# A split activation tile, two more load buffers, a new order of K pairs and exchanged bank kinds in the down projection of a decoder layer

## The chip, the core and the metric

One core of one Trainium2 chip computes one layer of a hybrid decoder for 256 tokens. The metric is the device time of one execution in microseconds, as the median of several. TensorE (PE in the profile) multiplies, VectorE (DVE) and ScalarE (ACT) prepare operands and drain results, GpSimd (POOL) moves small pieces by DMA, and SyncE (SP) issues the weight loads.

## The reference

All arrays are float32. Sizes: 256 tokens, width 2048, feed-forward width 5632. The layer has four parts:

```python
z = rms_norm(x, mix_norm_g) @ w_in                 # 2048 -> 8208, feeds mLSTM heads and forgetting attention
x = x + concat([A, B]) @ w_out                     # 2048 -> 2048
u = rms_norm(x, ffn_norm_g) @ w_up                 # 2048 -> 2 * 5632
a, g = split(u, 2)
a = causal_dwconv(a, conv_w, conv_b)               # width 3
x = x + (gelu(a) * g) @ w_down                     # 5632 -> 2048
gate = sigmoid(rms_norm(x, ple_norm_g) @ w_ple_gate)
x = x + gate * (p @ w_ple_proj)
```

The change touches the last three products: up, down, and gate with proj.

## The kernel before

**Products in three matmuls.** Each float32 operand is kept as a rounded part (hi) and the rest (lo), both in the type fp32r. A product is hi x hi, hi x lo and lo x hi, three matmuls into one PSUM bank (lines 996 to 998 for down, 1235 to 1237 for up, 311 to 313 for the gate). Weights arrive as raw float32 tiles of 128 x 1024; ACT casts hi (line 947), DVE subtracts it for lo (line 948). This pair of steps is a *split* (`part`, line 946).

**Activations.** The transposed, split activations are tiles `aT` of 16 K tiles x 512 columns (hi 256, lo 256). `new_aT` (line 357) gives them out from one pool with two slots: `hT`, `catT`, `x2T`, `uA`, then `w2`, then `x3T`, so `w2` takes the slot of `x2T`, the input of up, and `x3T` that of `uA`.

**Units.** From the up stage on everything runs as a list of units (`Unit`, line 922; `run_units`, line 953). A unit has loads (SP), a split, and matmuls. Loads are issued as long as raw buffers are free (`free_raws`, `new_raw`), splits as long as pairs of hi and lo buffers are. Up has 11 groups of 16 units (`up_group`), one unit per K tile, 12 matmuls each. Its result is drained to `EZ` by ACT (line 853), transposed by DVE into `Y` (line 191), moved back to `EZ` by 16 POOL DMAs (line 197), and goes through the convolution, GELU and gate product in pieces hung behind later units (`up_act`, lines 865 to 880); the last group's pieces run behind units 5 to 9 of down.

**Down.** Each half of 1024 output columns goes through 44 K tiles in 22 pairs (`down`, line 977). A *plain* pair is two units (`eight`) of one load and 12 matmuls. A *seven-product* pair (`seven`, for the nine pairs of `SEVEN`) does a 2 x 2 block product with seven products instead of eight: two loads, four units of 3, 6, 6 and 6 matmuls, four 512-wide subtractions in place on the raw tiles (lines 1044, 1045, 1054, 1055), and sums of the left blocks, S, that were written to DRAM in the up stage and are loaded again (line 1027). Its two raw tiles are free only after its fourth split. The plain products of a half are gathered in four banks (`X_tag`), P1, P5, P6 and P7 in four others (`P_tag`); `sums_done` adds the latter to the residual behind the last seven-product pair, `add_rest` the former at the end.

**Buffers.** In the up stage there are 3 raw tiles and 4 pairs of hi and lo. From the first unit of down on there are also: raw `pT` (one, from the pool of the left sums), and, once the last convolution has left them, `EZ` (two) and a part of `Y` (`ring`, one); and in `w2` three more pairs of hi and lo and two places for S. PSUM has 8 banks, 4 of the kind "mm" and 4 of "aux". Up groups alternate between the kinds, down exchanges them between its halves, and the gate and proj products and the transposes of `x3T` use one kind each.

**Order.** The program order is not the final one on an engine: a scheduler reorders instructions within the dependencies when the program is built. Each engine then works its list in order, and so does SP's queue.

Of the kernel before, what the change touches and what calls it, by code (L numbers as in the profile page):

```python
# [9 lines left out]
F32 = mybir.dt.float32  # L10
F32R = mybir.dt.float32r
# [4 lines left out]
P = 128  # L16
S = 256
NT = S // P
D = 2048
KD = D // P  # L20
# [4 lines left out]
KF = FF // P  # L25
# [6 lines left out]

BLK = 1024
RAW, PARTS = 3, 4
PARTS2 = 3

SEVEN = (2, 4, 6, 8, 10, 12, 14, 16, 18)
AHEAD_DMA, AHEAD_SPLIT = 3, 3
PAD = 16


LO_SHIFT = 16
LAST_UP = 9


@with_exitstack
def layer_kernel(
# [19 lines left out]
    def bank(tag, name):  # L67
        return ps.tile([P, 512], F32, tag=tag, name=name)
# [283 lines left out]
        act.copy(dst, b[:, 256:512])  # L352
        dve.tensor_add(dst, b[:, 0:256], dst)

    aT = {}

    def new_aT(name):
        aT["cur"] = apool.tile([P, KD, 512], F32R, tag="aT", name=name, bufs=2)
        return aT["cur"]

    all_k = list(range(0, KD, 2))

# [438 lines left out]
    with tc.tile_pool(name="ffn", bufs=1) as fp:  # L801
# [98 lines left out]
        def new_raw(j, name):  # L900
            tag = free_raws(j)[0]
            taken.append(tag)
            used[tag] = len(used) and max(used.values()) + 1
            if tag == "ring":
                return ring[:, 0:2].rearrange("p a b -> p (a b)")
            if tag in ("e0", "e1"):
                return EZ[:, int(tag[1])]
            if tag == "raw":
                return wp.tile([P, BLK], F32, tag="raw", name=name, bufs=RAW)
            return fp.tile([P, BLK], F32, tag=tag, name=name, bufs=room[tag])  # L910

        def new_parts(j, shift):
# [40 lines left out]
        def run_units(us, first_late, gate):  # L953
            loaded = split = 0
            for i, u in enumerate(us):
                if i == first_late:
                    w2 = new_aT("w2").rearrange("p k n -> p (k n)")
                    v = w2[:, 0 : 6 * BLK].rearrange("p (u n) -> p u n", n=BLK)
                    room.update(pT=1, e0=1, e1=1, ring=1)
                    late.update(gate=gate, free=i + LAST_UP, hi=v[:, 0:3], lo=v[:, 3:6],  # L960
                                S=w2[:, 6 * BLK :].rearrange("p (b i c) -> p b i c", b=2, c=256))
                more = i >= first_late
                now[0] = i
                while True:
# [12 lines left out]
        def down(c0, X_tag, P_tag, sums_done, done, at):  # L977

            banks, seen, us = {}, {}, []
            pairs = range(KF // 2)
            plain = [p_ for p_ in pairs if p_ not in SEVEN]
            total = {"P1": len(SEVEN), "P5": len(SEVEN), "P6": len(SEVEN), "P7": len(SEVEN)}
            for t in range(NT):
                for n in range(2):
# [80 lines left out]

            for p_ in pairs:
                if p_ in SEVEN:
                    us.extend(seven(p_, sums_done if p_ == SEVEN[-1] else None))  # L1070
# [57 lines left out]
        def x3_columns(*ks):  # L1128
            return lambda *_: [column(x3s[k // 4], k % 4, get_x3T()[:, k], g_ple[:, k : k + 1]) for k in ks]

        def transposes(*ks, tag="aux"):
            return lambda *_: [transpose_x(get_x3T(), k0, g_ple, tag) for k0 in ks]

        pT = {}
# [41 lines left out]
        def last_group(c0, n):  # L1176
# [44 lines left out]
        def up_group(q):  # L1221
# [29 lines left out]
        us += down(1024, "aux", "mm", sums_done(1024), add_rest(1024),  # L1251
                   {23: x3_squares(0), 27: x3_squares(1),
                    31: x3_columns(0, 1, 2, 3), 35: x3_columns(4, 5, 6, 7)})
# [48 lines left out]
```

## Time and profile before

| | |
|---|---|
| median of three runs | 1263.54 us (1263.43 to 1263.77) |
| profiled execution | 1263.79 us, span 1262.1 us |
| mean granted TensorE clock | 0.997 |
| DMA | 271.27 MB, 215 GB/s on average |
| matmuls of up, by line 1235 | 704, 389 ns each as listed (they overlap) |

Rows of a time line give start, duration, engine, line, operation and out<-in; in brackets the idle time before the instruction and what ended it. "x4" merges four neighbours. Rows by stretch give, after the stretch, its length, then busy us (and instructions) of PE, PEld (weight load), DVE, ACT and POOL, the granted clock, the busy share of the 16 DMA engines and GB/s. SPq rows are issues of DMAs. Since matmuls overlap, the distance between starts says more than the duration.

### The profile page before, as it was taken

The page shows a single profiled execution, that of the slowest core. Times are in us where ns is not written, and L with a number is a line of the kernel's source. Part 1 is how long each engine was busy: PE and PEld are TensorE (multiplying, and loading weights), DVE is VectorE, ACT ScalarE, POOL GpSimd, SP SyncE. Part 2 cuts the span into 40 slices and gives each one's busy share as a digit, 9 for nine tenths or more (in the row PEclk, how much of TensorE's full clock was granted, in tenths as well). Part 3 has the DMA queues.
Part 4 walks back from the last instruction along what each step waited for, and adds up shares of the span by engine and source line. Part 5 has one row for each costly group of instructions (what it writes and reads, how often), then busy time and mean ns, then how long its engine had stood idle before and what let it go on. Part 6 is the DMA issues. An engine that isn't in the chain of part 4 may idle for free.

```text
span 1262.1 us, 16487 instructions
## 1 busy us (share of the span) xinstructions
PE 1247.4 (99%) x5887; PEld 1051.9 (83%) x5887; DVE 831.6 (66%) x1055; ACT 684.1 (54%) x964; POOL 210.4 (17%) x395
## 2 busy tenths in 40 slices
PE   9999999999999999999999999999998999999998
PEld 7899988888888788888888888888876888888887
DVE  6455668744565645665676567657668998899653
ACT  7655555545454544665565556546545555556542
POOL 2003035100213202202211220222020000050000
PEclk9999999999999999999999999999998999999999
DMA  8667767656666757777877887787786785877670
GB/s 257 183 181 207 222 189 203 198 157 171 200 194 214 210 182 218 210 231 211 253 219 219 244 233 225 226 235 232 228 238 234 256 325 190 263 249 232 190 237 35
DMA packets 133476, 271.27 MB, mean 215 GB/s; under 512 B 14007, under 2 KB 28977, under 8 KB 133393
## 3 DMA queue, kind: packets, MB, share of 16 engines
q1 hardware_dynamic: 119936, 246.51, 64.8%
q0 software_dynamic: 13072, 23.53, 6.4%
q8 instruction: 46, 0.75, 0.3%
q14 instruction: 37, 0.30, 0.1%
q10 hardware_dynamic: 385, 0.16, 0.0%
HBM read 246.54 MB, written 6.83 MB: 201 GB/s over the span
## 4 chain that ended last, share of the span: by engine, by line
PE 94%; DMA 2%; DVE 2%; ACT 1%; issue 0%; SPq 0%; ACTq 0%; DVEq 0%
PE up L1235 13%; PE up L1237 13%; PE up L1236 13%; PE tg L312 10%; PE tg L311 10%; PE tg L313 10%; PE wg L343 5%; PE wg L344 2%; DMA raw<-in_w_down_dram 1%; PE dnP L997 1%; PE dnP L998 1%; PE dnP L996 1%; PE dn(0, 1)_8857 L996 1%; PE dn(0, 0)_8853 L996 1%; PE dn(1, 0)_8861 L996 1%; PE dn(1, 0)_8861 L998 1%
## 5 line engine op out<-in xcount | busy, mean ns | idle before, releaser
L948 DVE TENSOR_TENSOR lo<-raw,hi 128x1024 fp32r<-128x1024 f32 x235 | 284.4, 1214 | 185.7 <-ACT hi L947 185.0
L947 ACT CAST hi<-raw 128x1024 fp32r<-128x1024 f32 x235 | 244.3, 1045 | 247.5 <-DMA raw<-in_w_up_dram 118.5
L282 DVE TENSOR_TENSOR lo<-raw,hi 128x1024 fp32r<-128x1024 f32 (+2 forms) x161 | 178.2, 1112 | 149.1 <-ACT hi L280 148.8
L1237 PE MATMUL up<-hi,x2T 128*128 128x512 f32 x704 | 273.9, 389 | 0.0
L1236 PE MATMUL up<-lo,x2T 128*128 128x512 f32 x704 | 273.9, 389 | 0.0
L1235 PE MATMUL up<-hi,x2T 128*128 128x512 f32 x704 | 269.6, 389 | 1.3 <-DVE x2T L139 1.3
L280 ACT CAST hi<-raw 128x1024 fp32r<-128x1024 f32 (+2 forms) x161 | 153.7, 960 | 150.3 <-PE tg L313 77.5
L1235 PEld LDWEIGHTS up<-hi,x2T 128*128 128x128 f32 x704 | 132.2, 188 | 28.8 <-DVE x2T L139 1.5
L1237 PEld LDWEIGHTS up<-hi,x2T 128*128 128x128 f32 x704 | 132.1, 188 | 27.6
L1236 PEld LDWEIGHTS up<-lo,x2T 128*128 128x128 f32 x704 | 132.1, 188 | 27.4
L312 PE MATMUL tg<-lo,hT 128*128 128x512 f32 (+1 forms) x384 | 136.8, 357 | 0.0
L311 PE MATMUL tg<-hi,hT 128*128 128x512 f32 (+1 forms) x384 | 135.6, 358 | 0.0
L313 PE MATMUL tg<-hi,hT 128*128 128x512 f32 (+1 forms) x384 | 135.5, 354 | 0.0
L197 POOL DMA_DIRECT2D EZ<-Y x176 | 93.1, 536 | 171.1 <-DVE Y L191 140.0
L343 PE MATMUL wg<-hT,hi 128*128 128x512 f32 x256 | 90.2, 399 | 0.0
L312 PEld LDWEIGHTS tg<-lo,hT 128*128 128x128 f32 x384 | 72.2, 188 | 7.7 <-DVE lo L282 0.5
L313 PEld LDWEIGHTS tg<-hi,hT 128*128 128x128 f32 x384 | 72.1, 188 | 7.5
L311 PEld LDWEIGHTS tg<-hi,hT 128*128 128x128 f32 x384 | 71.7, 188 | 7.1
L344 PE MATMUL wg<-hT,lo 128*128 128x256 f32 x256 | 70.1, 283 | 0.0
L947 ACT CAST w<-raw 128x1024 fp32r<-128x1024 f32 (+1 forms) x41 | 40.5, 998 | 34.0 <-DMA raw<-in_w_down_dram 12.6
L948 DVE TENSOR_TENSOR w<-raw,w 128x1024 fp32r<-128x1024 f32 (+1 forms) x41 | 46.9, 1153 | 14.2 <-ACT w L947 14.0
L343 PEld LDWEIGHTS wg<-hT,hi 128*128 128x128 f32 x256 | 47.5, 188 | 9.1
(633 smaller groups left out, 1963.0 us busy)
## 6 DMA issues: line engine op xcount, KB each, us to landing
raw<-in_w_up_dram SPq DMA_DIRECT2D x176, 512.0 KB, 4.9
raw<-in_w_in_dram SPq DMA_DIRECT2D x79, 512.0 KB, 4.1
raw<-in_w_down_dram SPq DMA_DIRECT2D x55, 512.0 KB, 6.3
raw<-in_w_in_dram SPq DMA_DIRECT2D x48, 344.0 KB, 3.5
raw<-in_w_out_dram SPq DMA_DIRECT2D x32, 512.0 KB, 4.7
EZ<-Y POOLq DMA_DIRECT2D x176, 64.0 KB, 5.4
EZ<-in_w_down_dram SPq DMA_DIRECT2D x22, 512.0 KB, 5.9
raw<-in_w_ple_gate_dram SPq DMA_DIRECT2D x20, 512.0 KB, 5.3
```

The source lines that it names most:

```text
L280: act.copy(hi, raw[:, :w])
L282: dve.tensor_sub(lo, raw[:, :w], f32(hi))
L311: pe.matmul(o, ah, hi[:, i, :], start=first, stop=False)
L312: pe.matmul(o, ah, lo[:, i, :], start=False, stop=False)
L313: pe.matmul(o, al, hi[:, i, :], start=False, stop=last)
L343: pe.matmul(o, h[:, i, cols], a, start=first, stop=False)
L344: pe.matmul(o[:, 256:512], l[:, i, cols], a[:, 0:256], start=False, stop=last)
L947: act.copy(hi, raw)
L948: dve.tensor_sub(lo, raw, f32(hi))
L1235: pe.matmul(o, ah, hi[:, n], start=k == 0, stop=False)
L1236: pe.matmul(o, ah, lo[:, n], start=False, stop=False)
L1237: pe.matmul(o, al, hi[:, n], start=False, stop=k == KD - 1)
```

## The change

- `aT` tiles are made of two tiles, K tiles 0 to 11 (tag `aTa`) and 12 to 15 (`aTb`), each with two slots (class `Tiles`).
- `w2` takes a slot of `aTa` alone: two pairs of hi and lo (`PARTS2` 2 instead of 3) and two places for S.
- A slot of `aTb` becomes two raw buffers of the new tag `late`, from the first unit of down to the end.
- The first half of down goes through its pairs in the order `FIRST`, with the plain pairs 0, 1, 3, 5 ahead of the first seven-product pair; the second half keeps its order. `last7` names the pair behind which `sums_done` runs.
- The bank kinds "mm" and "aux" are exchanged from the first up group on, through down, the transposes of `x3T`, `pT`, gate and proj.
- `EZ` and `ring` may be used as raw buffers from one unit later.

```diff
-PARTS2 = 3
+PARTS2 = 2
+FIRST = (0, 1, 3, 5, 2, 7, 4, 6, 9, 8, 11, 10, 13, 12, 15, 14, 17, 16, 19, 18, 20, 21)
+FRONT = 12
...
-        aT["cur"] = apool.tile([P, KD, 512], F32R, tag="aT", name=name, bufs=2)
-        return aT["cur"]
+    class Tiles:
+        def __init__(self, name):
+            self.a = apool.tile([P, FRONT, 512], F32R, tag="aTa", name=name, bufs=2)
+            self.b = apool.tile([P, KD - FRONT, 512], F32R, tag="aTb", name=name + "b", bufs=2)
+        def __getitem__(self, idx):
+            k = idx[1]
+            if isinstance(k, slice):
+                v, o = (self.a, 0) if k.stop <= FRONT else (self.b, FRONT)
+                k = slice(k.start - o, k.stop - o)
+            else:
+                v, o = (self.a, 0) if k < FRONT else (self.b, FRONT)
+                k -= o
+            return v[(idx[0], k, *idx[2:])]
...
+            if tag == "late":
+                if tag not in late:
+                    late[tag] = apool.tile([P, 2, BLK], F32, tag="aTb", name="w2raw", bufs=2)
+                    late["n"] = 0
+                late["n"] += 1
+                return late[tag][:, late["n"] % 2]
...
-                    w2 = new_aT("w2").rearrange("p k n -> p (k n)")
-                    v = w2[:, 0 : 6 * BLK].rearrange("p (u n) -> p u n", n=BLK)
-                    room.update(pT=1, e0=1, e1=1, ring=1)
-                    late.update(gate=gate, free=i + LAST_UP, hi=v[:, 0:3], lo=v[:, 3:6],
-                                S=w2[:, 6 * BLK :].rearrange("p (b i c) -> p b i c", b=2, c=256))
+                    v = apool.tile([P, 6, BLK], F32R, tag="aTa", name="w2", bufs=2)
+                    room.update(late=2, pT=1, e0=1, e1=1, ring=1)
+                    late.update(gate=gate, free=i + LAST_UP + 1, hi=v[:, 0:2], lo=v[:, 2:4],
+                                S=v[:, 4:6].rearrange("p b (i c) -> p b i c", c=256))
...
-        def transposes(*ks, tag="aux"):
+        def transposes(*ks, tag="mm"):
...
-            bk = bank("aux", "pTp")
+            bk = bank("mm", "pTp")
...
-                    st[key] = bank("mm", f"tl{t}{c}")
+                    st[key] = bank("aux", f"tl{t}{c}")
...
-                        st["b"] = {(t, n): bank("mm" if q % 2 else "aux", f"up{t}{n}") for n in range(2) for t in range(NT)}
+                        st["b"] = {(t, n): bank("aux" if q % 2 else "mm", f"up{t}{n}") for n in range(2) for t in range(NT)}
...
-        us += down(0, "mm", "aux", sums_done(0), add_rest(0), {})
-        us += down(1024, "aux", "mm", sums_done(1024), add_rest(1024),
+        us += down(0, "aux", "mm", sums_done(0), add_rest(0), {}, FIRST)
+        us += down(1024, "mm", "aux", sums_done(1024), add_rest(1024),
...
-            g_ = (units(token_group(w_ple_gate, all_k, get_x3T, c0, n, gate_done(c0, n)))
+            g_ = (units(token_group(w_ple_gate, all_k, get_x3T, c0, n, gate_done(c0, n), tag="aux"))
...
-            p_ = units(token_group(w_ple_proj, [0], lambda: pT["t"], c0, n, proj_done, tag="aux"))
+            p_ = units(token_group(w_ple_proj, [0], lambda: pT["t"], c0, n, proj_done, tag="mm"))
```

More of the change, by code (lines that the diff above doesn't have):

```diff
@@ L353, in merge @@
         dve.tensor_add(dst, b[:, 0:256], dst)
-    aT = {}
+    class Tiles:
[11 more added lines that the diff above has]
+            return v[(idx[0], k, *idx[2:])]
     def new_aT(name):
-        aT["cur"] = apool.tile([P, KD, 512], F32R, tag="aT", name=name, bufs=2)
-        return aT["cur"]
+        return Tiles(name)
     all_k = list(range(0, KD, 2))
@@ L975, in run_units, with down @@
                 u.fn(*u.parts)
-        def down(c0, X_tag, P_tag, sums_done, done, at):
+        def down(c0, X_tag, P_tag, sums_done, done, at, pairs):
             banks, seen, us = {}, {}, []
-            pairs = range(KF // 2)
             plain = [p_ for p_ in pairs if p_ not in SEVEN]
+            last7 = [p_ for p_ in pairs if p_ in SEVEN][-1]
             total = {"P1": len(SEVEN), "P5": len(SEVEN), "P6": len(SEVEN), "P7": len(SEVEN)}
@@ L1069, in down @@
                 if p_ in SEVEN:
-                    us.extend(seven(p_, sums_done if p_ == SEVEN[-1] else None))
+                    us.extend(seven(p_, sums_done if p_ == last7 else None))
                 else:
@@ L1249, in layer_kernel @@
         first_late = len(us)
-        us += down(0, "mm", "aux", sums_done(0), add_rest(0), {})
-        us += down(1024, "aux", "mm", sums_done(1024), add_rest(1024),
+        us += down(0, "aux", "mm", sums_done(0), add_rest(0), {}, FIRST)
+        us += down(1024, "mm", "aux", sums_done(1024), add_rest(1024),
                    {23: x3_squares(0), 27: x3_squares(1),
-                    31: x3_columns(0, 1, 2, 3), 35: x3_columns(4, 5, 6, 7)})
+                    31: x3_columns(0, 1, 2, 3), 35: x3_columns(4, 5, 6, 7)}, range(KF // 2))
         for c0, n in ((0, 512), (512, 512), (1024, 512), (1536, 512)):
-            g_ = (units(token_group(w_ple_gate, all_k, get_x3T, c0, n, gate_done(c0, n)))
+            g_ = (units(token_group(w_ple_gate, all_k, get_x3T, c0, n, gate_done(c0, n), tag="aux"))
                   if c0 < D - n else last_group(c0, n))
-            p_ = units(token_group(w_ple_proj, [0], lambda: pT["t"], c0, n, proj_done, tag="aux"))
+            p_ = units(token_group(w_ple_proj, [0], lambda: pT["t"], c0, n, proj_done, tag="mm"))
             if c0 == 0:
```

## The prediction

> **What bounds the kernel now.** I read the page first, then busy time by stretches, then the instructions of each engine around the two stretches in which TensorE is not full.
>
> ```profile
> span 1262.1 us, 16487 instructions
> PE 1247.4 (99%) x5887; PEld 1051.9 (83%) x5887; DVE 831.6 (66%) x1055; ACT 684.1 (54%) x964; POOL 210.4 (17%) x395
> ...
> 400.00:500.00 100.00, 98.45 (x437) 80.98 (x437) 53.69 (x57) 47.09 (x60) 21.32 (x40) 1.00 0.70 207
> ...
> 900.00:950.00 50.00, 46.99 (x202) 37.40 (x201) 36.44 (x43) 26.81 (x32) 9.04 (x17) 1.00 0.77 233
> 950.00:1000.00 50.00, 45.56 (x184) 35.86 (x184) 43.71 (x53) 26.47 (x30) 0.00 (x0) 0.93 0.75 256
> 1000.00:1050.00 50.00, 50.00 (x222) 41.40 (x221) 45.16 (x51) 29.34 (x37) 0.00 (x0) 1.00 0.74 261
> ```
>
> PE is busy 1247.4 of 1262.1 us, so the change can only win what lies in gaps and at a slow clock. The rows by stretch place them: 1.55 us at the start of the up stage (400 to 500), and 3.01 + 4.44 us between 900 and 1000, where the granted clock (third figure from the end) also drops to 0.93. From 1000 on PE is full again. The instructions show the same in time:
>
> ```profile
> 434.26 0.39 PE L313 MATMUL tg<-hi,catT 128*128 128x512 f32 x1
> 434.94 1.25 PE L147 MATMUL xT<-ident,xs 128*128 128x128 f32 x8 [0.29 <-DVE xs L769]
> 437.45 0.50 PE L1235 MATMUL up<-hi,x2T 128*128 128x512 f32 x1 [1.26 <-DVE x2T L139]
> ...
> 916.30 0.39 PE L996 MATMUL dn(0, 0)_7993<-hi,uA 128*128 128x512 f32 x1
> 916.53 0.39 PE L997 MATMUL dn(0, 0)_7993<-lo,uA 128*128 128x512 f32 x1
> ...
> 939.76 0.50 PE L996 MATMUL dn(0, 0)_7993<-w,uA 128*128 128x512 f32 x1 [0.69 <-ACT w L947]
> ...
> 955.19 0.57 PE L996 MATMUL dn(1, 1)_8005<-hi,uA 128*128 128x512 f32 x1 [1.82 <-ACT hi L947]
> 956.14 1.22 PE L996 MATMUL dnP<-w 128*128 128x512 f32 x2 [0.38 <-ACT w L947]
> ...
> 958.86 0.41 PE L996 MATMUL dn(0, 0)_7993<-hi,uA 128*128 128x512 f32 x1
> ...
> 968.57 0.49 PE L996 MATMUL dnP<-hi,uB 128*128 128x512 f32 x1 [2.01 <-ACT hi L947]
> ...
> 1043.03 0.39 PE L996 MATMUL dn(0, 0)_8853<-hi,uA 128*128 128x512 f32 x1
> ...
> 1156.59 0.39 PE L311 MATMUL tg<-w,x3T 128*128 128x512 f32 x1
> ```
>
> Matmuls of 512 columns start 0.227 us apart (916.30, 916.53). Both halves of the down projection hold the same 9 x 21 + 13 x 24 = 501 of them. The second takes 1156.59 - 1043.03 = 113.56 us, which is 501 x 0.227: it loses nothing. The first takes 1043.03 - 916.30 = 126.73: it loses **13.2 us**, of which 7.45 are gaps and the rest slow matmuls behind them. Six matmuls from 956.14 to 958.86 take 2.72 us instead of 1.36 after the gap of 1.82: about 1.4 us per long gap.
>
> Why the first half starves stands in ACT's casts and SP's loads:
>
> ```profile
> 935.98 0.62 ACT L947 CAST w<-raw 128x512 fp32r<-128x512 f32 x1 [3.01 <-DMA raw<-in_w_down_dram]
> 954.09 1.04 ACT L947 CAST hi<-raw 128x1024 fp32r<-128x1024 f32 x1 [2.86 <-DVE w L948]
> 967.90 0.62 ACT L947 CAST hi<-EZ 128x512 fp32r<-128x512 f32 x1 [5.46 <-DMA EZ<-in_w_down_dram]
> ...
> 920.16 0.33 SPq L933 DMA_DIRECT2D raw<-in_w_down_dram  x1
> 930.35 1.60 SPq L933 DMA_DIRECT2D raw<-in_w_down_dram  x2
> ...
> 934.68 0.38 SPq L1027 DMA_DIRECT2D w<-sums  x1
> 942.77 0.33 SPq L933 DMA_DIRECT2D raw<-in_w_down_dram  x1
> ```
>
> SP issues nothing from 920.16 to 930.35 and from 934.68 to 942.77: only four raw buffers exist then, and a seven-product pair holds two until its fourth split. The casts then wait for data (3.01, 5.46), and around 954 for VectorE, which does the last convolution beside the splits.
>
> **The change part by part.** Prices of the pieces, and the rows that set when they start:
>
> ```profile
> 905.42 0.39 PE L1235 MATMUL up<-hi,x2T 128*128 128x512 f32 x1
> 905.48 0.35 SPq L933 DMA_DIRECT2D raw<-in_w_down_dram  x1
> 910.68 0.33 SPq L933 DMA_DIRECT2D raw<-in_w_down_dram  x1
> 914.79 2.41 ACT L853 ACTIVATE EZ<-up,rstd_ffn 128x512 f32<-128x512 f32 x4
> 919.32 4.24 POOL L197 DMA_DIRECT2D EZ<-Y  x8 [7.20 <-DVE Y L191]
> 930.25 2.64 POOL L197 DMA_DIRECT2D EZ<-Y  x5 [0.40 <-DMA EZ<-Y]
> 938.66 1.99 ACT L947 CAST w<-raw 128x1024 fp32r<-128x1024 f32 x2 [2.07 <-DMA raw<-in_w_down_dram]
> 939.74 2.36 DVE L948 TENSOR_TENSOR w<-raw,w 128x1024 fp32r<-128x1024 f32 x2 [0.39 <-ACT w L947]
> 951.03 0.69 DVE L1045 TENSOR_TENSOR raw<-raw,raw 128x512 f32<-128x512 f32 x1
> 951.64 1.27 DVE L873 SCALAR_TENSOR_TENSOR Y<-Y,cT 128x255 f32<-128x255 f32 x3
> ...
> raw<-in_w_down_dram SPq DMA_DIRECT2D x26, 512.0 KB, 5.7
> EZ<-Y POOLq DMA_DIRECT2D x16, 64.0 KB, 7.1
> ```
>
> From these rows: two casts take 1.99 us, so one is 1.05 alone and 0.95 back to back; a 1024-wide subtraction 1.22 and 1.14; a 512-wide one 0.69 and 0.61; a convolution step 0.40. A load lands 5.7 us after issue, a move of EZ 7.1.
>
> *Bank kinds.* The first up group takes the banks of the output projection instead of those of the eight transposes. In the built order 18 up matmuls (4.1 us) now stand ahead of these transposes, and the residual adds that free the last two banks end long before. So the up stage starts at 434.26 + 0.23 instead of 437.45: 2.96 us, less 1.25 for the transposes, which are still made, and about 0.1 for breaking up the matmuls: **1.6 won**. Bounds: 0, if the first weights or banks come late, and 1.7. In all later stages both kinds are exchanged together, which changes no release: nothing.
>
> *Sums loads moved.* Two loads of sums now stand in SP's queue, behind the first and the second load of down, where they wait for TensorE to leave K tile 11 of the last up group (905.42). Behind them is the load of 905.48, some 0.4 us late; its data lands at 911.6, and PE wants it at 919.0: cast and subtraction (2.2 us) still fit with 5 us over. Nothing.
>
> *Plain pairs first, two more raws, split tiles.* Eight plain units give PE 96 x 0.227 = 21.8 us, to 938.1, of which each needs one load and one cast and subtraction (2.72 us of PE against 1.14 of DVE). The hi and lo buffers of the w2 tile come free at 905.4 and not at 916.3, the two new raws at 916.3, and each free buffer takes a load. So six loads go out from 916 to 923 and the first seven-product pair (wanted 938.1) has landed near 926: no stall to 948.3, where pair 4 begins. The starvation at 930 to 945 is gone.
>
> What is late next: pairs 4 and 6 follow each other, and the last convolution falls among their splits. PE begins pair 4 at 948.3 and has 39 matmuls in the built order, 8.8 us, until it wants the third product of pair 6, at 957.1. Its cast waits for a subtraction before which DVE has, from the first split of pair 4 on, 8 half-wide steps, 8 convolution steps and 7 wide ones (two of them the gate product and the lo part of uC): 8 x 0.6 + 8 x 0.4 + 7 x 1.14 = 16.0 us. ACT copies EZ behind the cast of the fourteenth unit, which waits for PE to leave the eighth (938.1 + 0.2 + 0.95), so from 939.2; the first split of pair 4 can reach DVE at 940.8. So DVE is there at 956.8, some 0.7 later with ACT's answers between, and the cast ends at 958.6: a stall of **1.5 us**.
>
> The copy of EZ (L865) must wait for EZ's moves, however. The cast of the fourth unit of down now precedes the four evictions of up (914.79) on ACT, and waits for its load (910.68 + 5.7 = 916.4). The evictions and all behind them, DVE's two transposes and POOL's moves, come up to 2.6 us later. The last move, issued until 932.9 now, landed at about 940 by the row, and would then at 942: the copy is 0 to 2.7 us late and the stall 1.5 to 4.2. I take 3.0, nearer the middle since the 7.1 is a median over moves that share the engines with more loads than the last five do. Behind it come 0.5 (the next cast in ACT's order ends 0.95 later, PE has 2 matmuls of 0.227 meanwhile) and an allowance of 0.4 for the first load into EZ, which leaves when the gate product has read EZ, about 953, and is wanted at 960.3. With 1.4 of slow clock the first half loses 3.0 + 0.5 + 0.4 + 1.4 = 5.3, so **7.9 won**; with the ends of the stall, and none or two stretches of slow clock, 2.4 to 7.9 lost. Bounds of the whole part: 13.2 won, and 0.
>
> On that clock: the Trainium skill, "TensorE: Matmul & The Clock Gate", section "What's actually happening", has the slow clock come after an idle window of about 3.4 us. The rows here show it after 1.82, so they do not agree with it. By the page the coming stalls would cost no clock; the sum would be 1.4 lower, an estimate of 1252.6.
>
> *Six buffer pairs instead of seven.* A seven-product pair and a plain one are six units, 45 matmuls, 10.2 us; DVE needs 5 x 1.14 + 5 x 0.61 = 8.75 back to back, and 5 x 1.22 + 5 x 0.69 = 9.55 with each alone. Each buffer pair then serves the same unit of the next period: between PE's leaving a plain unit and its need a period later lie 10.2 - 2.7 = 7.5 us, for 2.2 of cast and subtraction and the steps queued ahead of it on DVE. Nothing; rival 4 prices the contrary. *Pair 18* of the first half now has four units behind it, 10.9 us, not six, until the second half wants its banks; now they are read in about 6:
>
> ```profile
> 1025.55 1.22 DVE L1098 TENSOR_TENSOR xs<-dnP,xs 128x1024 f32<-128x1024 f32 x1 [0.26 <-PE dnP L998]
> ...
> 1030.16 1.22 DVE L1099 TENSOR_TENSOR xs<-dnP,xs 128x1024 f32<-128x1024 f32 x1
> ```
>
> Nothing. In the gate stages PE waits nowhere, and more raws only load earlier.
>
> Sum, against the profiled execution of 1263.79 us (1.7 around its span, 0.25 above the median): 1263.8 - 1.6 - 7.9 = 1254.3, and **1254.0** beside the median.
>
> **The rivals.** (1) *Nothing is left to wait for:* the order covers the convolution too. For it: 32 us without a stall ahead; against: 16.0 us of DVE work from 940.8, for PE's 8.8 from 948.3. 1263.8 - 1.6 - 13.2 = 1249.0, the floor.
> (2) *The stall moves:* pairs 4 and 6 each find their data late, as at 955 and 968 now. Two gaps of 2 with 1.4 of slow clock each and three of 0.7 make 8.9: 1263.8 - 1.6 - 4.3 = 1257.9.
> (3) *It does not do what it says:* the loads only queue, since the DMA share is 0.75 already; then only the up start is won, 1262.1. Against: SP stands idle for want of buffers, not of transfers, and while PE waits the share has room (0.54):
>
> ```profile
> 940.00:950.00 10.00, 8.24 (x33) 5.96 (x33) 8.65 (x11) 6.97 (x10) 0.00 (x0) 1.00 0.54 178
> ```
>
> (4) *Slower: six pairs are too few.* Place: the alternating pairs, 7 periods in the first half and 9 in the second. If one wide subtraction of 1.22 per period comes after PE, 16 x 1.22 = 19.5 are lost against 9.5 won: 1274. It decides from 9.5 / 16 = 0.6 us per period, just what DVE has over at the prices alone (10.2 - 9.55). For it: DVE is busy 45.16 of 50 us there; against: those 7.5 us, and no gap at all from 1000 to 1050 now.
>
> **How the numbers follow.** Forecast (2.4 to 7.9 lost, so 1251 to 1256.9) 0.50; rival 1 0.17, rival 2 0.16, rival 3 0.08, rival 4 0.09. 0.2% is 2.5 us, what a measurement of this kernel can tell from no change. Faster: 0.50 + 0.17 + 0.16 = 0.83; same 0.08; slower 0.09. The range holds the first three, from just below the floor to rival 2 with one more long gap: 1248.6 to 1260.5.
>
> **What would show it.** Right: the first up matmul directly behind the output projection, transposes after 18 of them; the first half of down 116 to 122 us long, full to about 948, with one long gap near 957 behind a cast that waits for DVE; the second half 113.6. Wrong: gaps before 948 on a load (rival 3), gaps spread over 1000 to 1150 behind lo subtractions (rival 4), a gate stage with waits, or evictions of the last up group that hold back something wanted before 938.

## The result, and the profile after

| | before | changed |
|---|---|---|
| median of four runs, us | 1263.49 (1261.48 to 1263.77) | 1255.59 (1255.10 to 1257.89) |
| profiled execution / span, us | 1263.79 / 1262.1 | 1255.10 / 1253.4 |
| last matmul of the output projection to first of down | 482.04 | 479.86 |
| first half of down, us (113.56 without a loss) | 126.73 | 119.77 |

The ratio is 0.9945, with a 95% interval of 0.9927 to 0.9962: faster by 0.4 to 0.7%. First the page of the changed kernel, and busy time by stretches (stretch, length, then PE, PEld, DVE, ACT, POOL, granted clock, DMA share, GB/s):

```profile
span 1253.4 us, 16510 instructions
PE 1243.8 (99%) x5887; PEld 1051.4 (84%) x5887; DVE 832.2 (66%) x1055; ACT 684.9 (55%) x964; POOL 210.4 (17%) x395
...
400.00:450.00 50.00, 50.00 (x226) 41.45 (x225) 30.23 (x38) 26.09 (x38) 13.01 (x25) 1.00 0.71 214
900.00:950.00 50.00, 49.18 (x217) 40.31 (x216) 35.94 (x44) 26.29 (x31) 9.05 (x17) 1.00 0.85 263
950.00:1000.00 50.00, 47.83 (x198) 37.96 (x199) 48.27 (x55) 30.31 (x34) 0.00 (x0) 0.97 0.84 277
1000.00:1050.00 50.00, 50.00 (x223) 41.38 (x222) 45.14 (x51) 27.94 (x35) 0.00 (x0) 1.00 0.75 255
```

The 1.55 us at the start of up are gone, and of the 7.45 between 900 and 1000 there are 2.99 left. PE's instructions in time:

```profile
434.69 0.39 PE L315 MATMUL tg<-hi,catT 128*128 128x512 f32 x1
434.91 0.39 PE L1256 MATMUL up<-hi,x2T 128*128 128x512 f32 x1
...
439.00 0.60 PE L149 MATMUL xT<-ident,xs 128*128 128x128 f32 x4
...
914.55 0.39 PE L1017 MATMUL dn(0, 0)_7999<-hi,uA 128*128 128x512 f32 x1
...
950.34 0.50 PE L1018 MATMUL dnP<-w 128*128 128x512 f32 x1 [1.15 <-DVE w L970]
...
952.81 0.50 PE L1017 MATMUL dn(1, 0)_8007<-hi,uA 128*128 128x512 f32 x1 [1.28 <-ACT hi L969]
...
954.28 0.50 PE L1017 MATMUL dn(0, 0)_7999<-hi,uAb 128*128 128x512 f32 x1 [0.45 <-ACT hi L969]
...
954.86 0.63 PE L1018 MATMUL dn(1, 0)_8007<-lo,uA 128*128 128x512 f32 x1
955.29 0.63 PE L1019 MATMUL dn(1, 0)_8007<-hi,uA 128*128 128x512 f32 x1
...
958.26 0.39 PE L1019 MATMUL dn(0, 0)_7999<-hi,uAb 128*128 128x512 f32 x1
...
1034.32 0.39 PE L1017 MATMUL dn(0, 0)_8862<-hi,uA 128*128 128x512 f32 x1
```

Up now starts 0.22 us behind the output projection, with the transposes after 18 of its matmuls. The first half of down runs from 914.55 to 1034.32 and is full to 949; its three gaps lie within 5 us, and the eight matmuls from 954.86 to 958.26 stand 0.43 apart instead of 0.227. It still loses 119.77 - 113.56 = 6.2. Listed durations overlap, so a gap costs more than is listed for it: by the distances between starts the three cost 1.43, 1.56 and 0.78 us, the slow matmuls 1.6, and three later steps without a listed gap 0.65, together 6.0. The profiled executions differ by 8.69: 482.04 - 479.86 = 2.18 at the start of up and 126.73 - 119.77 = 6.96 in the first half, less 0.43 by which this execution was late already at its last output projection matmul (434.69 against 434.26), make 8.71.

What stands in ACT, DVE and SP around the gaps:

```profile
903.87 0.35 SPq L1048 DMA_DIRECT2D w<-sums  x1
904.74 0.42 SPq L1048 DMA_DIRECT2D w<-sums  x1
...
917.56 2.42 ACT L869 ACTIVATE EZ<-up,rstd_ffn 128x512 f32<-128x512 f32 x4
941.02 1.06 ACT L881 COPY Y<-EZ 128x1024 f32<-128x1024 f32 x1 [0.69 <-DMA EZ<-Y]
...
946.10 1.66 DVE L889 SCALAR_TENSOR_TENSOR Y<-Y,cT 128x255 f32<-128x255 f32 x4
947.68 0.68 DVE L1075 TENSOR_TENSOR w2raw<-w2raw,raw 128x512 f32<-128x512 f32 x1
948.28 0.86 DVE L889 SCALAR_TENSOR_TENSOR Y<-Y,cT 128x254 f32<-128x254 f32 x2
949.07 1.21 DVE L970 TENSOR_TENSOR w<-raw,w 128x1024 fp32r<-128x1024 f32 x1
...
950.77 1.06 ACT L895 ACTIVATE Y<-Y 128x1024 f32<-128x1024 f32 x1 [3.45 <-DVE Y L889]
951.73 1.03 ACT L969 CAST hi<-w2raw 128x1024 fp32r<-128x1024 f32 x1
```

The subtraction that PE waits for at 950.34 is that of 949.07, the third product of pair 4. In front of it on DVE stand the last convolution's steps; behind it ACT sits 3.45 us on the GELU, which needs the last of these steps, and the cast behind the GELU ends the second gap.

### The profile page after: what moved, and what is told of

It reads as the page before. It is cut to its first block, busy times and chain, and to the rows that moved or that the text cites. A ratio compares the mean times of both kernels' runs of the same rounds, so it can differ in the third digit from the quotient of the medians.

```text
span 1253.4 us, 16510 instructions
## 1 busy us (share of the span) xinstructions
PE 1243.8 (99%) x5887; PEld 1051.4 (84%) x5887; DVE 832.2 (66%) x1055; ACT 684.9 (55%) x964; POOL 210.4 (17%) x395
## 4 chain that ended last, share of the span: by engine, by line
PE 95%; DMA 2%; DVE 1%; ACT 1%; issue 1%; POOL 0%; SPq 0%; DVEq 0%; ACTq 0%
PE up L1257 13%; PE up L1258 13%; PE up L1256 13%; PE tg L314 10%; PE tg L313 10%; PE tg L315 10%; PE wg L345 5%; PE wg L346 2%; DMA EZ<-Y 1%; PE dnP L1018 1%; PE dnP L1019 1%; PE dnP L1017 1%; PE dn(1, 0)_8870 L1018 1%; PE dn(0, 1)_8866 L1018 1%; PE dn(0, 1)_8866 L1017 1%; PE dn(0, 0)_8862 L1018 1%
## 5 line engine op out<-in xcount | busy, mean ns | idle before, releaser
L970 DVE TENSOR_TENSOR lo<-raw,hi 128x1024 fp32r<-128x1024 f32 (+1 forms) x219 | 264.4, 1209 | 181.9 <-ACT hi L969 181.6
L969 ACT CAST hi<-raw 128x1024 fp32r<-128x1024 f32 (+1 forms) x219 | 227.3, 1041 | 236.7 <-DMA raw<-in_w_up_dram 126.9
L1258 PE MATMUL up<-hi,x2T 128*128 128x512 f32 x528 | 205.5, 389 | 0.0
L1257 PE MATMUL up<-lo,x2T 128*128 128x512 f32 x528 | 205.4, 389 | 0.0
L1256 PE MATMUL up<-hi,x2T 128*128 128x512 f32 x528 | 204.8, 389 | 0.0
L1256 PEld LDWEIGHTS up<-hi,x2T 128*128 128x128 f32 x528 | 99.1, 188 | 20.6
L1258 PEld LDWEIGHTS up<-hi,x2T 128*128 128x128 f32 x528 | 99.1, 188 | 20.5
L314 PE MATMUL tg<-lo,hT 128*128 128x512 f32 (+1 forms) x288 | 102.9, 357 | 0.0
L313 PE MATMUL tg<-hi,hT 128*128 128x512 f32 (+1 forms) x288 | 101.8, 358 | 0.0
L315 PE MATMUL tg<-hi,hT 128*128 128x512 f32 (+1 forms) x288 | 101.7, 354 | 0.0
L1257 PE MATMUL up<-lo,x2Tb 128*128 128x512 f32 x176 | 68.5, 389 | 0.0
L1258 PE MATMUL up<-hi,x2Tb 128*128 128x512 f32 x176 | 68.5, 389 | 0.0
L1256 PE MATMUL up<-hi,x2Tb 128*128 128x512 f32 x176 | 65.2, 389 | 0.0
L315 PEld LDWEIGHTS tg<-hi,hT 128*128 128x128 f32 x288 | 54.1, 188 | 5.5
L313 PEld LDWEIGHTS tg<-hi,hT 128*128 128x128 f32 x288 | 53.7, 188 | 5.4
```

The lines of the kernel that those rows point to most:

```text
L313: pe.matmul(o, ah, hi[:, i, :], start=first, stop=False)
L314: pe.matmul(o, ah, lo[:, i, :], start=False, stop=False)
L315: pe.matmul(o, al, hi[:, i, :], start=False, stop=last)
L969: act.copy(hi, raw)
L970: dve.tensor_sub(lo, raw, f32(hi))
L1256: pe.matmul(o, ah, hi[:, n], start=k == 0, stop=False)
```

## The experiments

"First half" is the first half of down in the profiled execution. One caution: the kernel before and the first experiment hold down's instructions in the same order, and their first halves are 126.73 and 124.90; a difference below 2 us of single profiles decides nothing by itself. Each ratio is taken against executions of the kernel before that were timed beside that experiment, whose medians lie between 1262.8 and 1263.5 us, so the ratios compare better across rows than the medians.

| kernel | pair order | buffer pairs | S loads at | late raws | first half | median | ratio, 95% interval |
|---|---|---|---|---|---|---|---|
| before | old | 7 | 918 | no | 126.7 | 1263.5 | 1 |
| bank kinds alone | old | 7 | 918 | no | 124.9 | 1260.23 | 0.9976, 0.9964 to 0.9987 |
| old order | old | 6 | 905 | yes | 125.7 | 1262.95 | 0.9993, 0.9982 to 1.0005 |
| new order, buffers of before | new | 7 | 918 | no | 125.6 | 1262.55 | 0.9998, 0.9985 to 1.0011 |
| no late raws | new | 6 | 903 | no | 120.9 | 1257.31 | 0.9943, 0.9924 to 0.9963 |
| w2 and S late | new | 6 | 916 | no | 122.2 | 1258.75 | 0.9966, 0.9955 to 0.9978 |
| S late | new | 6 | 918 | no | 125.7 | 1261.01 | 0.9986, 0.9977 to 0.9996 |
| seven pairs, S late | new | 7 | 917 | no | 128.9 | 1264.45 | 1.0013, 1.0003 to 1.0022 |
| changed | new | 6 | 904 | yes | 119.8 | 1255.59 | 0.9945, 0.9927 to 0.9962 |

All but the first row have the bank kinds exchanged. S stands for the sums of the left blocks, a late raw for one of the two new load buffers.

**Bank kinds alone.** The exchange, in the kernel before:

```diff
-                        st["b"] = {(t, n): bank("mm" if q % 2 else "aux", f"up{t}{n}") for n in range(2) for t in range(NT)}
+                        st["b"] = {(t, n): bank("aux" if q % 2 else "mm", f"up{t}{n}") for n in range(2) for t in range(NT)}
```

and so for down, transposes, gate and proj.

> The kernel before with the exchange of the bank kinds alone. The forecast's step (up matmuls stand ahead of the eight transposes): 1.6 to 2.2 us under the kernel before (1261.3 to 1261.9), all of it between the last output projection matmul and the first of down; the first half of down still loses 13 us. If the exchange had a part in the stalls of down (banks of the first half come free earlier or later), the first half would lose clearly less than 13 and the time would go below 1260.5.

From the last output projection matmul to the first of down it takes 479.87, as in the changed kernel: 2.17 won. The time is 0.13 to 0.36% lower (1.6 to 4.5 us). But 1260.23, and a first half that loses 11.3 and not 13, are also the sign that was set for the exchange having a part in the stalls of down. The traces show no such part: the instructions stand in the same order, the evictions of the last up group begin 1.52 us ahead of down's first matmul in both, and every listed gap of the first half ends with a cast or a subtraction. The traces part where the casts of down wait for their loads, and this one has no stretch of slow matmuls. With one profile of each, whether the 1.8 are chance stays open.

**The old order of pairs in the changed kernel.**

```diff
-        us += down(0, "aux", "mm", sums_done(0), add_rest(0), {}, FIRST)
+        us += down(0, "aux", "mm", sums_done(0), add_rest(0), {}, range(KF // 2))
```

> The changed kernel with the old order of the pairs in the first half (0, 1, 2, 3 ...); late raws, six pairs of hi and lo and bank kinds as changed. Theory (both the order and the raws are needed): the two raws take away the waits for data at 939 to 945, those behind the last convolution stay, so the first half loses 8 to 10 us and the time is 1257 to 1260. Rival, the raws alone do it: the time of the changed kernel, 1255.5 within 1. Rival, the order alone does it: about 1261.3, the first half loses 12 to 13.

A miss, slower than the theory: nothing is left of the gain of down, and the rival for which the order is all fits better. There are six gaps between 951 and 970 and two later; the longest:

```profile
968.94 0.50 PE L1017 MATMUL dnP<-w,uC 128*128 128x512 f32 x1 [3.71 <-ACT w L969]
```

So the buffers without the order bring nothing.

**No late raws.**

```diff
-                    room.update(late=2, pT=1, e0=1, e1=1, ring=1)
+                    room.update(pT=1, e0=1, e1=1, ring=1)
```

> The changed kernel without the two late raws (six pairs of hi and lo, new order, bank kinds kept). Theory (both are needed): four raws let the loads of pairs 4 and 6 go out only when pair 2 gives its two raws back, about 937, so casts wait for data near 945 to 955 and the first half loses 8 to 10 us: 1257 to 1260. Rival, the order alone does it: 1255.5 within 1, no cast of pair 4 waits for a load. Rival, the raws alone do it: about 1261.3.

The time, 1257.31, lies at the edge of the theory's range; the trace is nearer the rival. Two casts of pair 4 do wait for their loads, 0.82 and 2.71 us, but the subtraction behind the second comes only 0.1 later, counted from down's first matmul, than in the changed kernel. PE is full to 949, and the gaps are those of the changed kernel:

```profile
949.99 0.50 PE L1018 MATMUL dnP<-w 128*128 128x512 f32 x1 [1.28 <-DVE w L970]
...
952.46 0.80 PE L1017 MATMUL dn(1, 0)_8004<-hi,uA 128*128 128x512 f32 x1 [1.29 <-ACT hi L969]
```

The two raws are worth 1.1 us in the profile, below what one profile tells, and the intervals of the two kernels lie on each other. The stretch of slow matmuls behind these gaps is 5.3 us long here and 3.4 in the changed kernel, which is where most of the 1.1 lies.

**The new order with the buffers of before** (`FIRST` and `last7` in the kernel before, with the bank kinds exchanged).

> The kernel before with bank kinds exchanged and the new order of pairs, with its seven pairs of hi and lo and its four raws. Beside the run without late raws it prices the seventh pair of buffers: by the forecast (six pairs cost nothing) the two agree within 1 us; if six pairs were too few, this one is faster by 2 us or more and its second half is no shorter than 113.6 only in the other.

It is 5 us slower than the kernel without late raws, and as slow as before. The second half is the same in both (113.33; the 113.78 of the six-pair kernels holds two gate matmuls, which moved ahead of down's last ones), so six pairs cost nothing there; but something in the split tile or the number of pairs is worth as much as the order. The next three runs look for it.

**w2 and S late.** In the kernel without late raws the last up group takes K tiles 12 to 15 first, so that the slot of w2 comes free with its last matmul:

```diff
+            ks = list(range(KD)) if q < KF // 4 - 1 else [*range(FRONT, KD), *range(FRONT)]
...
-            return [unit(k) for k in range(KD)]
+            return [unit(k) for k in ks]
```

> The kernel without late raws, in which only the last up group goes through its K tiles as 12 to 15, 0 to 11, so that the slot that w2 takes comes free with the last up matmul (about 914.5) and not at about 904. Its brother without that edit has a first half of 120.9 us and 1257.3; the kernel with the same order of pairs but w2 on a whole tile has 125.6 and 1262.6. Theory (the early release of w2's slot is what the new order needs, and the seventh buffer pair is not what matters): first half 124 to 126, 1260 to 1263. Rival (the release is hidden, and the difference of those two lies in the number of buffer pairs or in EZ's first use): first half 120 to 122, 1256 to 1258.

Nearer the rival. The late slot costs 1.3 us in the profile, with overlapping intervals. The edit also turns ACT's order: the cast that needs the late slot stands behind the evictions of the last up group, which start at 912.58 and not at 916.36.

**S late** (in the kernel without late raws, two places for S in the slot of K tiles 12 to 15, the rest of w2 as it was), and **the seventh pair** on top of it:

```diff
-                                S=v[:, 4:6].rearrange("p b (i c) -> p b i c", c=256))
+                                S=apool.tile([P, 2, BLK], F32R, tag="aTb", name="w2S", bufs=2).rearrange("p b (i c) -> p b i c", c=256))
...
-PARTS2 = 2
+PARTS2 = 3
...
-                    late.update(gate=gate, free=i + LAST_UP + 1, hi=v[:, 0:2], lo=v[:, 2:4],
+                    late.update(gate=gate, free=i + LAST_UP + 1, hi=v[:, 0:3], lo=v[:, 3:6],
```

> The kernel without late raws (first half 120.9) with the two places for S moved to the slot of K tiles 12 to 15, so that S is loaded at about 914 to 917 and not at 904; six pairs of hi and lo. It differs from the kernel with seven pairs and S late (first half 128.9) in the seventh pair alone, and from the one without late raws in the time of the S loads alone. Theory (the seventh pair turns the order of the loads and costs the 7): 120.5 to 122.5, 1257 to 1259. Rival (two loads of 0.5 MB among the crowded transfers of 917 to 935 cost it): 125 to 129, 1261 to 1265.

> The kernel without late raws, with a third pair of hi and lo in w2's slot (seven pairs again) and the two places for S in the slot of K tiles 12 to 15 (so S is loaded when up ends, about 914, and not at 904). Of the two kernels with the new order and four raws, that with seven pairs on a whole tile has a first half of 125.6 us, that with six on the split tile 120.9; the late release of w2 with late S loads gave 1.3 of the 4.7 between them. Theory A (the seventh pair changes which loads stand ahead in SP's queue and makes the rest): 123.5 to 126, 1260 to 1262.5. Theory B (the seventh pair is harmless, the release of w2 and S is all): 120.5 to 122.5, 1257 to 1259.

S late makes 4.8 us (120.9 to 125.7, intervals apart): the rival of that expectation holds. The time of the S loads is not quite all that differs, since the build also exchanges two of ACT's casts ahead of the evictions, which come 0.7 later. The stretches show why the loads cost (columns as above; first the kernel without late raws, with its cast of pair 2's second split, then the one with S late):

```profile
920.00:925.00 5.00, 5.00 (x24) 4.14 (x23) 3.44 (x4) 2.81 (x3) 4.10 (x8) 1.00 0.87 283
925.00:930.00 5.00, 5.00 (x24) 4.14 (x23) 3.15 (x4) 0.76 (x2) 3.53 (x8) 1.00 0.98 259
930.00:935.00 5.00, 5.00 (x24) 4.14 (x23) 4.03 (x5) 2.63 (x3) 0.85 (x2) 1.00 0.86 243
...
930.50 2.00 ACT L969 CAST w<-raw 128x1024 fp32r<-128x1024 f32 x2 [2.16 <-DMA raw<-in_w_down_dram]
```

```profile
920.00:925.00 5.00, 5.00 (x23) 4.14 (x23) 3.52 (x4) 2.47 (x3) 3.35 (x7) 1.00 1.03 352
925.00:930.00 5.00, 5.00 (x23) 4.14 (x23) 1.30 (x2) 0.14 (x1) 1.18 (x3) 1.00 1.03 247
930.00:935.00 5.00, 5.00 (x23) 4.13 (x22) 2.61 (x3) 1.53 (x2) 3.96 (x8) 1.00 1.03 265
...
917.92 0.90 SPq L1048 DMA_DIRECT2D w2S<-sums  x2
...
929.86 1.05 ACT L969 CAST hi<-raw 128x1024 fp32r<-128x1024 f32 x1 [5.00 <-DMA raw<-in_w_down_dram]
...
935.42 2.00 ACT L969 CAST w<-raw 128x1024 fp32r<-128x1024 f32 x2 [1.91 <-DMA raw<-in_w_down_dram]
...
937.79 0.50 PE L1018 MATMUL dn(0, 0)_7997<-w,uA 128*128 128x512 f32 x1 [0.77 <-DVE w L970]
```

Two transfers of 0.5 MB issued at 917.92 fall among weight loads and the moves of EZ; the DMA engines are then full from 920 to 935, and a cast waits 5.00 for its load, where none between 915 and 940 waits over 2.6 in the kernel without late raws. Pair 2's second split is cast at 935.42 and not at 930.50, and PE's first gap, at 937.79, waits for its subtraction. Issued at 903 the two transfers stand ahead of the crowd.

The seventh pair costs another 3.2 (128.9 against 125.7, intervals apart): the direction of theory A of its run, but 128.9 and 1264.45 lie above the numbers of both theories. In the built order of its SP queue the load of the thirteenth unit stands ahead of the second tile of pair 2, and pair 2's second split waits for that tile until 937.66, which the six-pair kernel casts at 935.42 (the tile is the eleventh load of down, issued at 925.82, and the tenth there, at 925.20). How much of the 3.2 this one wait makes is not shown:

```profile
930.71 1.05 ACT L969 CAST hi<-raw 128x1024 fp32r<-128x1024 f32 x1 [6.18 <-DMA raw<-in_w_down_dram]
932.36 0.62 ACT L969 CAST hi<-raw 128x512 fp32r<-128x512 f32 x1 [0.59 <-DMA raw<-in_w_down_dram]
937.66 1.04 ACT L969 CAST hi<-raw 128x1024 fp32r<-128x1024 f32 x1 [4.69 <-DMA raw<-in_w_down_dram]
```

That w2 and S late together cost less than S late alone goes with the evictions, 4.5 us earlier there (912.58 against 917.11) and the EZ moves with them. The table holds the comparison twice. With S late, six pairs have a first half of 122.2 where the evictions precede the cast of the fourth unit and 125.7 where they stand behind it; seven pairs have 125.6 (the new order with the buffers of before) and 128.9. So in both the early evictions go with 3.3 to 3.5 us, and in both the seventh pair costs 3.2 to 3.4. The early ones also get w2 later, which cannot be what helps them; other differences of these builds are not excluded. The changed kernel, whose evictions stand behind that cast, was not run with them ahead of it.

**What the rest is: without the taps of the last convolution** (the last 512 channels lack taps 1 and 2).

```diff
-                    for d in (1, 2):
+                    for d in (1, 2) if q < KF // 4 - 1 else ():
```

> The changed kernel without the eight convolution steps of the last up group on VectorE (taps 1 and 2 of its last 512 channels are left out; ScalarE's part of it stays). Theory (what is left is VectorE's work on the last convolution ahead of the splits of pairs 4 and 6): the gaps at 950 and 953 go, the first half is 113.6 to 115, the time 5 us under the changed kernel, 1250 to 1251. Rival (two seven-product pairs in a row are too much for VectorE by themselves): gaps of 1 us and more stay between 948 and 965, first half 117 to 119.

1249.46 in its one execution, 0.5 below the theory's range (0.6 of its lead over the changed kernel's profile lies before up); the gaps at 950 and 953 go, as the theory has it. One gap is left, and the first half, from 913.97 to 1028.67, loses 1.1 us:

```profile
953.92 0.73 PE L1017 MATMUL dnP<-hi,w 128*128 128x512 f32 x2 [0.35 <-ACT hi L969]
...
1028.67 0.39 PE L1017 MATMUL dn(0, 0)_8854<-hi,uA 128*128 128x512 f32 x1
```

Eight steps, 3.2 us of DVE, are 5.1 of the 6.2 us that the changed kernel still loses. With them goes the place of the GELU, which the build now puts ahead of a cast of pair 4.

**Pairs kept apart.**

```diff
-FIRST = (0, 1, 3, 5, 2, 7, 4, 6, 9, 8, 11, 10, 13, 12, 15, 14, 17, 16, 19, 18, 20, 21)
+FIRST = (0, 1, 3, 5, 2, 7, 4, 9, 6, 11, 8, 13, 10, 15, 12, 17, 14, 19, 16, 18, 20, 21)
```

> The changed kernel with a plain pair between each two seven-product pairs after the first four plain ones (0 1 3 5 2 7 4 9 6 11 8 ...; 16 and 18 now follow each other at the end of the half). Theory (the gaps start at pair 4's own third and fourth product, so the neighbour matters only for what follows): the first gap of about 1.2 at 950 stays, the second at 953 shrinks; first half 117 to 119, 1253 to 1254.5. Rival of the forecast's own ledger (the stall belongs to pair 6 behind pair 4): all gaps go, 113.6 to 115, 1250. Slower, if 16 and 18 in a row make a new gap at about 1020.

1254.04, ratio 0.9922 (0.9903 to 0.9941). Matmuls of the second half moved ahead of the end of the first, so both halves are taken together: 232.78 us, against 233.56 in the changed kernel. The gap of the third product at 950 is gone, one of 1.28 at 951.29 and one of 0.77 at 964.68 are there; the time is the theory's, but neither theory nor rival holds cleanly, since the first gap was to stay or all to go. No gap near 1020.

**The EZ moves of the last group on ScalarE's queue**, to bring the copy of EZ forward.

```diff
-                pool.dma_start(out=c[32 * b : 32 * b + 32, a::4], in_=y[32 * a : 32 * a + 32, :, b])
+                q.dma_start(out=c[32 * b : 32 * b + 32, a::4], in_=y[32 * a : 32 * a + 32, :, b])
...
-            move(y, Z)
+            move(y, Z, act if q == KF // 4 - 1 else pool)
```

> The changed kernel with the 16 moves of EZ of the last up group issued by ScalarE's queue, not GpSimd's. Theory (the copy of EZ at 941 is late because the moves leave from 922 to 935): the moves have left by 925 and landed by 932, ScalarE's copy comes by 933 to 936, the convolution runs under the plain pairs and the gaps at 950 and 953 shrink to 1 us together or go: first half 113.6 to 117, 1250 to 1253. Rival (the copy's place in ScalarE's order holds it, or VectorE's total work does): the copy stays near 940, 1255 to 1256.

A plain miss, 1263.42:

```profile
922.05 15.51 ACTq L199 DMA_DIRECT2D EZ<-Y  x16
937.89 1.04 ACT L969 CAST hi<-raw 128x1024 fp32r<-128x1024 f32 x1 [16.77 <-DMA EZ<-Y]
...
938.99 0.80 PE L1017 MATMUL dn(0, 0)_7999<-hi,uA 128*128 128x512 f32 x1 [10.56 <-ACT hi L969]
```

The 16 issues take 15.51 us of ACT's time, during which it casts nothing, and PE stands 10.56 us. The issues themselves are 0.59 to 0.74 us each, 9.8 together; of the rest, 5.3 are five waits that the trace puts down to weight loads landing. GpSimd's 16 issues in the changed kernel span 13.0 us (922.09 to 935.05) and hold up no cast. The copy came at 942.20, no earlier, so the theory was not tested. In the kernel without late raws the copy came at 937.34 and the convolution no earlier, because the cast of 942.52, which waited 2.71 for its load, stands between them. Whether an earlier copy would help the changed kernel stays open.

**The convolution behind later splits.** On top of the pairs kept apart:

```diff
-LAST_UP = 9
+LAST_UP = 20
...
+                with tc.issue_after(newest[0].ins), tc.issue_after(newest[1].ins):
+                    hook()
...
-                at = (8, 9, 10, 11, 12, 13) if q < KF // 4 - 1 else (5, 6, 6, 7, 8, LAST_UP)
+                at = (8, 9, 10, 11, 12, 13) if q < KF // 4 - 1 else (5, 12, 13, 14, 18, 20)
```

(`newest` holds the latest split's cast and subtraction; `LAST_UP` is the unit of down behind which `EZ` and `ring` may be used as raws.)

> The changed kernel with the pairs kept apart (0 1 3 5 2 7 4 9 6 11 ...), in which the last convolution's steps are queued on ScalarE and VectorE behind the splits of the units 17, 18, 19, 23 and 25 of down, so that they no longer stand among the splits of pair 4. Theory (VectorE's place of the convolution costs the rest): both halves of down together 228 to 230 us (232.8 with the pairs apart alone, 227.1 without a loss), 1249.5 to 1251.5. Rival (the same work on VectorE is only late elsewhere, since VectorE is busy without a break there): 231 to 234, 1252.5 to 1255.5.

1255.12, both halves 233.41: the rival's numbers, by another way. No gap is left before 969.99; the loss has moved behind it, to a cast that waits for its load:

```profile
972.16 1.04 ACT L971 CAST w<-w2raw 128x1024 fp32r<-128x1024 f32 x1 [3.95 <-DMA w2raw<-in_w_down_dram]
...
974.20 0.79 PE L1018 MATMUL dn(1, 0)_8007<-hi,uB 128*128 128x512 f32 x1 [3.02 <-ACT hi L971]
```

EZ is free as a raw 11 units later here, and its first load goes out at 965.76 and not at 951.59. That this is the cause of the wait is a reading and not shown: in the next run EZ's first load goes out at 970.94, and no such wait comes.

**The taps on ScalarE and GpSimd**, with the order of the run before:

```diff
+                            act.activation(t, a_[:, j], AF.Copy, scale=cT[:, 88 - 44 * d + k : 89 - 44 * d + k])
+                            pool.tensor_add(c_[:, j, d:S], c_[:, j, d:S], t[:, : S - d])
...
```

> As the run before it, but the eight tap steps of the last convolution are taken from VectorE: ScalarE makes the scaled copies (eight more of its steps of 0.52) and GpSimd, idle from 935 on, adds them. Theory (VectorE's total in this stretch is what binds): 227.5 to 229 us for both halves, 1249 to 1250.5, as without the taps (228.5). Rival (GpSimd's adds are slow and hold back the GELU in ScalarE's queue, with casts behind it, or slow VectorE down): a gap of 1 us or more behind a cast between 955 and 975, 1252 to 1256.

Median 1254.0 (1250.64 to 1254.79), ratio 0.9921 (0.9906 to 0.9936); both halves 230.30, the shortest of all complete kernels, with gaps of 0.51 at 962.81 and 1.43 at 975.16, both behind a cast. The theory's 227.5 to 229 is missed by 1.3, and the time is in the rival's range. The profiled execution was late by 3 us before up began (its first up matmul at 437.85), which hides the shorter halves in its time. So this version and the one with the pairs apart beat the kernel before; that either beats the changed one is not shown, as the intervals overlap. GpSimd's adds are not free for DVE:

```profile
955.96 0.99 DVE L981 TENSOR_TENSOR lo<-raw,hi 128x512 fp32r<-128x512 f32 x1 [0.15 <-ACT hi L981]
956.99 1.01 DVE L1076 TENSOR_TENSOR raw<-raw 128x512 f32<-128x512 f32 x1
957.92 1.65 DVE L981 TENSOR_TENSOR w<-raw,w 128x1024 fp32r<-128x1024 f32 x1
...
955.49 0.91 POOL L896 TENSOR_TENSOR Y<-Y,tap 128x255 f32<-128x255 f32 x1 [0.77 <-ACT tap L895]
956.48 0.97 POOL L896 TENSOR_TENSOR Y<-Y 128x254 f32<-128x254 f32 x1
957.82 0.66 POOL L896 TENSOR_TENSOR Y<-Y 128x254 f32<-128x254 f32 x1 [0.38 <-ACT Y L895]
```

Beside them a half-wide subtraction takes 0.99 to 1.01 and not 0.69, a wide one 1.65 and not 1.22.

## Why the prediction was right, and where not

The time forecast was 1254.0 and came out at 1255.59, by its likeliest case: the start of up and about half of the first half's loss won, what is left at the last convolution. The two terms of the sum were off by 0.6 and 0.9 in opposite directions, so that the total is nearer than its parts is in part luck.

- *Bank kinds*: right in mechanism, mis-sized. 2.18 won, not 1.6: behind 18 matmuls the eight transposes cost about 0.8 (up takes 479.64 from first matmul to down, 2112 x 0.22667 are 478.7, and before lost 0.1 there too), not the 1.25 + 0.1 taken.
- *First half of down*: 6.96 won against 7.9, 6.2 lost against 5.3, within 2.4 to 7.9. One slow stretch of 8 x 0.2 = 1.6 us, where 1.4 was taken. The reading of the kernel before, in which all beyond its 7.45 of gaps were slow matmuls, was too simple: there eleven matmuls stand 0.43 apart, which is 2.2 us, and most of the rest is what each gap costs beyond its listed length.
- *The stall's place and form*: one pair too late, and not one long gap. It falls on the third and the fourth product of pair 4 at 950.34 and 952.81 and, with 0.45, on the second of pair 6, not as one gap on the third of pair 6 near 957. The copy of EZ came at 941.02, within the 939.2 to 941.9 allowed; the forecast let the late copy push the whole stall to the far end of DVE's work, while PE met the first convolution steps where they stand. That these are the cause is shown: without them 5.1 us go, and queued behind later splits they leave no gap before 969.99.
- *"Sums loads moved ... Nothing"*: this step failed. It priced the wait of 0.4 that the moved loads bring to the load behind them and not what they leave behind at 918. Moved back there in the kernel without late raws they cost 4.8 us; with w2 late too, and the evictions early, only 1.3.
- *Two more raws*: the forecast read the idle SP queue as a want of raw buffers, and laid the end of the starvation on plain pairs and raws together. With the plain pairs first and S early, four raws starve nothing; the raws' own share, 1.1 in the profiles, is not told from nothing.
- *Six pairs, "Nothing"*: no loss, as said (rival 4 shows no trace: no gap of down after 954.28); but with late S the step to six also wins, 3.2 and 3.4 us in two comparisons; in both the build with seven puts a later load ahead of pair 2's second tile. With S early it was not run.
- *Rivals*: 1 fell by the gaps at 950. 2 has something to it, since pair 4 waits 1.15 and 1.28 and pair 6 0.45, but 6.2 us are lost and not 8.9. 3 fell by the 7 us won in the first half, though of the raws alone it is as good as right. Two small slips change nothing: 1262.1 of rival 3 is 1262.2 by its own terms, and rival 2 with one more long gap of 2 + 1.4 is 1261.3 and not 1260.5. Of down's 7 us nothing comes from one part alone: the old order with the new buffers, and the new order with the old ones, each give all of it back.

## What to carry to other kernels

A part that is priced at nothing because its own wait is hidden may still move work out of a crowd: look at what the place that it leaves has to carry, in the DMA share by stretches. An idle issue queue says that buffers were lacking then, not that more buffers are the remedy; a changed order of consumers can remove the want. And where a stall is forecast behind a burst on one engine, look for it at the first consumer queued behind the burst's first step, not behind its last.

## What the runs showed of the hardware

- The slow matmuls at 954.86 to 958.26 stand 0.43 us apart for 3.4 us, then 0.23 again. The Trainium skill, "TensorE: Matmul & The Clock Gate", gives 426.7 ns for a cold 512-column matmul (section "Wait — 56ns, not 53.3ns?") and a window of about 3.4 us (section "What's actually happening"); spacing and length agree here. In other runs the length does not: such stretches last 2.1 and 2.6 us in the kernel before and 5.3 in the one without late raws. The idle window does not agree: the gaps in the 3.4 us ahead were 1.28 and 0.45. Nor does the length of one gap decide it in these runs: two gaps of 0.76 within 1.3 us (seven pairs, S late) are followed by a slow stretch of 3.0 us, one of 1.43 alone (taps on GpSimd) by none.
- DVE's slow subtractions beside GpSimd's adds (1.65 for 1.22): the Trainium skill, "Perfetto Trace Analysis", section "Optimizing Scalar/DVE Operations", says that the two share a read port and that moving work between them might not help. The slowing agrees; here the move shortened down nonetheless (230.30 against 233.41). In this trace the four subtractions that begin while an add has 0.4 to 0.6 us to run take 0.30 to 0.43 longer, and the four that begin ahead of an add they meet take their usual 1.22 to 1.23.
- An issue of a 64 KB move takes 0.61 us on ScalarE and 0.53 on GpSimd. Sixteen held ScalarE for 15.5 us, 5.3 of them in waits for weight loads to land.
- The last two experiments (the convolution behind later splits, then the taps on GpSimd) differ by 3.4 us before up, and all of it is there when these transposes, the same in both, begin:

```profile
10.43 0.60 PE L149 MATMUL xT<-ident,xs 128*128 128x128 f32 x4
...
13.82 0.60 PE L149 MATMUL xT<-ident,xs 128*128 128x128 f32 x4
```

Ahead of them the second one waits 1.22 us for a load at 7.81, and its matmuls of 512 columns then stand 0.43 apart, those of the first 0.23. From the first matmul of the tile wg (144.76 and 148.17) to the first up matmul (434.44 and 437.85) both take 289.68. So the length of a late stage is the better measure of a change there than the time of one execution.
